# Gate bias in nine rows, one transpose for the conv state, the sample tokens' output product in fp32, and an output norm in two passes

## The chip, the cores and the metric

The kernel runs on one core of one Trainium2 chip. The metric is the device time of one launch in microseconds (us); the figure to compare is the median of several launches of the compiled program. TensorE (PE) multiplies matrices out of SBUF into PSUM, VectorE (DVE), ScalarE (ACT) and GpSimd (POOL) work on tiles, and SyncE (SP) issues all of this kernel's transfers (DMA), one queue for the whole program.

## The reference

One step of one decoder layer with D = 1024, for a prompt of 512 tokens and for 8 sample sequences of 4 tokens with caches. Branch A is dilated window attention, branch B a gated delta rule with a short convolution ahead of it. What matters for this change:

```python
shift, scale, gate = jnp.split(jax.nn.silu(c) @ w_cond + b_cond, 3, axis=-1)   # c: 1 prompt row, 8 sample rows
h = x * (1 + scale[:, None]) + shift[:, None]
... = h @ w_in                                    # one projection; a part of it is qkv_b, 3 x 1024 columns
...
qkv_ext = concatenate([conv_state, qkv_b], axis=1)            # conv_state: 3 rows ahead of the tokens (zeros for the prompt)
qkv = silu(sum(qkv_ext[:, i:i + n] * w[i] for i in range(4)))
new conv_state = qkv_ext[:, -3:]                  # outputs conv_prompt (3, 3072) and conv_sample (8, 3, 3072)
...
merged = sigmoid(ga) * (ya @ w_branch_a) + sigmoid(gb) * (yb @ w_branch_b)
r = ALPHA * x + gate[:, None] * (merged @ w_out)
mu, var = mean(r), mean((r - mu) ** 2)            # over the 1024 columns of a row
out = (r - mu) * rsqrt(var + LN_EPS) * ln_g + ln_b
```

All arrays are float32.

## The kernel before

**How the order comes about.** The code does not issue instructions as it runs. It records them (`Recorder`), and a planner puts them in an order for each engine: it simulates the engines with a table of costs (`cost`), takes for an engine among the instructions that are ready the one of the lowest rank, then the one recorded first, and at the end `emit` issues everything in that order. That is why each row of the profile has line 724: rows are told apart by the names of their tiles (`out<-in`). A result counts as ready for the plan at its planned end plus `margin` (line 702): 0.1 us behind an instruction, 0.5 us behind a transfer. Pools of buffers decide when a tile can be written again. An instruction with `.at` is not planned ahead of that planned time. `rec.together()` keeps a group of instructions without others between. `rec.either` is a copy that goes to VectorE or ScalarE, whichever the plan has free.

**The stream.** The projection `h @ w_in` and the two branch products are a list of jobs, each with 128 columns of weights. The tokens (512 + 32 = 544) are the moving operand, in two halves of 272 columns. Weights and activations are split into a high and a low part (`hi`, `lo`; `hhi`, `hlo`) of the type fp32r, and each product is three: hi x hi, hi x lo, lo x hi, all added up in the PSUM tile `pp`. `wt` is a loaded weight tile, `ext` the evacuated result of a conv job. The other work of the layer runs as threads beside the stream, and its matmuls are put between those of the stream.

**The gate.** `gate_rows` (line 2007) computes the gate's third of `silu(c) @ w_cond + b_cond` in two halves of 512 columns. The weights `wg` come in eight loads. The product goes to `Y`; a matmul with the constant `sel` makes 73 rows of the 9 (prompt and 8 samples) in `pd`: those 9, then the samples' rows for their 32 tokens, twice. `grow` is loaded with the bias in 73 rows, VectorE adds `pd`, and `grow` is stored in DRAM (`dg`). At the end `gp` (the prompt's row on 128 partitions) and `gs` (64 x 1024, the samples' rows) are read back from `dg`.

**The conv state and the delta rule.** For each of 8 heads three conv jobs (q, k, v) run in the stream. Each copies its last three columns of the prompt and of the samples into `cx`; `delta_blocks` (line 1185) transposes `cx` in three pieces of 35 columns, copies the result to `crow`, and stores it with four transfers (one to `conv_p`, three to `conv_s`). In the same function scale factors of a head go through DRAM: `rrow` is stored as `dr` and read back by all partitions as `rb`. VectorE multiplies q and k of the head in `KQ` by scale factors from there, and TensorE transposes `KQ`. `rc` is a small tile of such factors that TensorE transposes earlier. `dblk`, `Ls`, `dtz` and `Tc` are later stations of the same head by way of DRAM (`Tb` is what `dtz` is stored from). `bias` is a tile of the position bias of the attention, which ScalarE exponentiates after its load (`bias_p`). `dO` and `rbo` are the same kind of round trip for the delta rule's output; `S` is its state, `KP` and `PTa` operands of the sample tokens' delta rule and attention, `slab` rows of the cache. `out_kv_s` are copies of caches from DRAM to DRAM, 16 rows at a time.

**The output.** The product with `w_out` runs over two halves of 512 columns (`wo0h`, `wo0l` and `wo1h`, `wo1l`: the halves' high and low parts, split from `wo`). For the prompt the merged activations are stationary (`mhi`, `mlo`), 128 tokens at a time, three products for each of 8 pieces; the last token tile goes in two steps of 256 columns. For the samples `ms` holds the high parts of 32 tokens and the low ones side by side, 64 stationary columns, and both are multiplied by `wo..h` and `wo..l`. In each half the order is: samples (tile 4), then token tiles 0 to 3. VectorE forms `r` = gate x product + ALPHA x `x` (the loaded piece `xr`), its statistics (`bn`, `mv`), and then the norm in five passes over `r` with the norm's weights `lng` and `lnb`, partly in one operation (`SCALAR_TENSOR_TENSOR`: subtract and multiply, or multiply and add) over 512 columns, or 768 for the last tile, partly in three single steps for the rest.

Of the kernel before, what the change touches and what calls it, by code (L numbers as in the profile page):

```python
# [19 lines left out]
D = 1024  # L20
KT = 8
# [224 lines left out]
class Recorder:  # L246
# [455 lines left out]
    def margin(self, p, op):  # L702
        return 0.1 if p.transfer is None else 0.5
# [73 lines left out]
def body(ctx, tc, io):  # L777
# [359 lines left out]
    def conv_job(h, s):  # L1137
# [4 lines left out]
        def begin():  # L1142
            if s == 1:
                hd.cx = dl.tile([128, 3, 35], F32, name="cx")
# [6 lines left out]
        def evac(n, ps):  # L1151
# [13 lines left out]
            ge.tensor_copy(cx[:, s, 0:3], ext[:, 512:515])  # L1165
            ge.tensor_copy(cx[:, s, 3:].rearrange("p (t b) -> p b t", b=8), es[:, :, 3:7])
# [18 lines left out]
    def delta_blocks(h):  # L1185
# [821 lines left out]
    def gate_rows():  # L2007

        sel = cst[:, CCOLS["selc"][0]:CCOLS["selc"][0] + 73]
        for n in range(2):  # L2010
            w = slice(512 * n, 512 * n + 512)
            wc = [op.tile([128, NT], F32, name="wg", tag="o")[:, 0:512] for _ in range(KT)]
            for k in range(KT):
                d = sp.dma_start(wc[k], io["w_cond"][128 * k:128 * k + 128, 2 * D + 512 * n:2 * D + 512 * n + 512])
                d.at = GATES[0] + (GATES[1] - GATES[0]) * (KT * n + k) / (2 * KT)
# [118 lines left out]

    def load_out(n):

        for k in range(0, KT, 2):
            raw = wraw.tile([128, 2, 512], F32, name="wo", tag="wraw")
# [208 lines left out]
```

## Time and profile before

| | |
|---|---|
| median of 3 runs | 930.28 us (930.02 to 931.19) |
| the profiled execution's own time | 931.52 us |
| its span, first to last instruction | 929.7 us |
| granted TensorE clock, mean | 0.988 |
| busy: TensorE, VectorE, ScalarE, GpSimd | 95%, 72%, 50%, 7% |
| matmul records, instructions in all | 8066, 20669 |
| moved | 238.37 MB, mean 256 GB/s |

The profile is of one execution. Times in its rows are us from the start of the span; the rows of a timeline give start, length, engine, operation, out<-in with shapes, and in brackets how long the engine stood idle just before and what it waited for. In the page's second part each digit stands for a fortieth of the span, 23.2 us, in tenths. Rows of the list of waits read: engine, tile it works on, what released it, total idle time, number of waits, longest. The chain of waits goes back from the last instruction and is printed in order of time. fp32 matmuls show more than one record for each instruction.

### The profile page before, as it was taken

The page shows a single profiled execution, that of the slowest core. Times are in us where ns is not written, and L with a number is a line of the kernel's source. Part 1 is how long each engine was busy: PE and PEld are TensorE (multiplying, and loading weights), DVE is VectorE, ACT ScalarE, POOL GpSimd, SP SyncE. Part 2 cuts the span into 40 slices and gives each one's busy share as a digit, 9 for nine tenths or more (in the row PEclk, how much of TensorE's full clock was granted, in tenths as well). Part 3 has the DMA queues.
Part 4 walks back from the last instruction along what each step waited for, and adds up shares of the span by engine and source line. Part 5 has one row for each costly group of instructions (what it writes and reads, how often), then busy time and mean ns, then how long its engine had stood idle before and what let it go on. Part 6 is the DMA issues. An engine that isn't in the chain of part 4 may idle for free.

```text
span 929.7 us, 20669 instructions
## 1 busy us (share of the span) xinstructions
PE 887.5 (95%) x8066; PEld 824.7 (89%) x8066; DVE 670.6 (72%) x1421; ACT 466.8 (50%) x1124; POOL 62.7 (7%) x176
## 2 busy tenths in 40 slices
PE   4899999899999999999999999999999999999995
PEld 1599998788999899989999989998899999989884
DVE  0574434575567999679998875637789799978768
ACT  0365468563568753568764666553352222234421
POOL 0120000010100100010110100102010000000000
PEclk9799999999999999999999999999999999999998
DMA  9678686575787969887888875549969899986713
GB/s 356 231 215 263 197 283 215 203 244 172 234 279 257 298 204 316 266 270 257 289 266 292 279 244 169 189 154 304 337 212 349 276 418 420 356 306 206 265 54 113
DMA packets 106766, 238.37 MB, mean 256 GB/s; under 512 B 31030, under 2 KB 62272, under 8 KB 103980
## 3 DMA queue, kind: packets, MB, share of 16 engines
q1 hardware_dynamic: 106668, 237.05, 75.4%
q8 instruction: 63, 1.03, 0.4%
q14 instruction: 35, 0.29, 0.1%
HBM read 220.69 MB, written 104.00 MB: 349 GB/s over the span
## 4 chain that ended last, share of the span: by engine, by line
PE 78%; DMA 11%; DVE 6%; ACT 2%; SPq 2%; issue 1%; DVEq 0%; ACTq 0%
PE pp L724 61%; PE pg L724 7%; PE pd L724 6%; PE pb L724 3%; DMA grow<-in_b_cond 2%; DMA wc<-in_w_cond 2%; SPq L724 2%; DMA out_kv_s<-in_cache 1%; DMA dtz<-Tb 1%; DMA bias<-in_bias_p 1%; DVE lo L724 1%; DMA rbo<-dO 1%; DVE acc L724 1%; DMA slab<-in_ks 1%; DVE r L724 1%
## 5 line engine op out<-in xcount | busy, mean ns | idle before, releaser
L724 PE MATMUL pp<-hhi,hi 128*128 128x272 f32 x1408 | 416.7, 296 | 7.6 <-ACT ext L724 3.1
L724 PE MATMUL pp<-hhi,lo 128*128 128x272 f32 x1408 | 416.6, 296 | 0.0
L724 PE MATMUL pp<-hlo,hi 128*128 128x272 f32 x1408 | 414.7, 295 | 0.2 <-DVE small L724 0.2
L724 PEld LDWEIGHTS pp<-hhi,hi 128*128 128x128 f32 x1408 | 267.2, 190 | 13.2 <-issue 4.1
L724 PEld LDWEIGHTS pp<-hlo,hi 128*128 128x128 f32 x1408 | 267.1, 190 | 2.9 <-issue 1.4
L724 PEld LDWEIGHTS pp<-hhi,lo 128*128 128x128 f32 x1408 | 266.7, 190 | 3.3 <-issue 2.1
L724 ACT ACTIVATE hi<-wt 128x1024 fp32r<-128x1024 f32 (+1 forms) x104 | 106.8, 1027 | 158.5 <-PE pp L724 117.9
L724 DVE TENSOR_TENSOR lo<-wt,hi 128x1024 fp32r<-128x1024 f32 (+1 forms) x104 | 122.8, 1180 | 57.2 <-ACT hi L724 51.0
L724 DVE SCALAR_TENSOR_TENSOR acc<-ext,cw,acc 128x568 f32<-128x568 f32 x72 | 57.7, 801 | 0.9 <-ACT acc L724 0.4
L724 ACT ACT_TABLE_LOAD x38 | 48.8, 1283 | 13.5 <-DMA cT<-in_cT 7.9
L724 DVE TENSOR_TENSOR slab<-slab 128x512 f32<-128x512 f32 (+1 forms) x66 | 42.9, 670 | 8.5 <-DMA slab<-in_ks 5.6
L724 DVE TENSOR_REDUCE slab<-slab 128x8 f32<-128x512 f32 (+2 forms) x66 | 43.0, 661 | 0.3
L724 ACT ACTIVATE zt<-pp 128x272 f32<-128x272 f32 x48 | 18.7, 390 | 38.2 <-PE pp L724 35.9
L724 PE MATMUL pp<-ybl,hi 128*128 128x272 f32 x128 | 36.9, 289 | 0.0
L724 PE MATMUL pp<-ybh,hi 128*128 128x272 f32 x128 | 36.9, 288 | 0.0
L724 PE MATMUL pp<-ybh,lo 128*128 128x272 f32 x128 | 36.6, 286 | 0.0
L724 ACT ACTIVATE P<-P,st 128x256 f32<-128x256 f32 (+1 forms) x64 | 31.2, 489 | 9.0 <-DVE st L724 8.8
L724 POOL COPY cx<-ext 128x3 f32<-128x3 f32 (+1 forms) x48 | 22.9, 506 | 117.7 <-ACT ext L724 117.7
L724 DVE TENSOR_TENSOR tmp<-Ls,Tb 32x15 f32<-32x15 f32 (+7 forms) x120 | 23.1, 193 | 5.5 <-DMA Ls<-dblk 2.2
L724 DVE CUSTOM_DVE_ANT_0 P<-pg,bias 128x256 f32<-128x256 f32 (+1 forms) x64 | 23.1, 400 | 5.4 <-PE pg L724 5.4
L724 ACT ACTIVATE spare<-pp 128x272 f32<-128x272 f32 (+1 forms) x32 | 16.0, 501 | 21.1 <-PE pp L724 21.0
L724 DVE TENSOR_TENSOR Tb<-Tb,tmp 32x15 f32<-32x15 f32 (+7 forms) x120 | 23.4, 195 | 4.1
(388 smaller groups left out, 1529.6 us busy)
## 6 DMA issues: line engine op xcount, KB each, us to landing
out_kv_s<-in_cache SPq DMA_DIRECT2D x144, 512.0 KB
wt<-in_w_in SPq DMA_DIRECT2D x88, 512.0 KB
out_kv_s<-in_cache SPq DMA_DIRECT2D x24, 496.0 KB
wc<-in_w_cond SPq DMA_DIRECT2D x8, 1024.0 KB
slab<-in_ks SPq DMA_DIRECT2D x32, 256.0 KB
slab<-in_vs SPq DMA_DIRECT2D x32, 256.0 KB
kv<-in_ks SPq DMA_DIRECT2D x16, 512.0 KB
kv<-in_vs SPq DMA_DIRECT2D x16, 512.0 KB
```

The source lines that it names most:

```text
L724: getattr(real[x.engine], x.name)(*map(arg, x.args), **{k: arg(v) for k, v in x.kw.items()})
```

## The change

Five things change, and the planner gives a new order for everything.

1. *Gate.* The bias comes as 9 rows (`brow`) into a tile that VectorE or GpSimd has set to zero before, loaded ahead of the weights `wg`. VectorE adds the product to it, the `sel` matmul repeats the sum as 73 rows, and these are copied to `grow` (`either`) and stored in `dg` as before.
2. *Conv state.* `cx` is [128, 81], one transpose, one copy, two stores.
3. *Margin.* A transfer's result counts as ready 1.0 us after its planned landing instead of 0.5.
4. *Samples' output product.* `ms` is [128, 8, 32] in fp32, copied by GpSimd. The product runs in one piece between the two halves: 8 x 4 matmuls of 32 stationary and 256 moving columns, each of the four on 32 rows of `pp` and its own column group of TensorE, with `w_out` unsplit. For this the first half of `w_out` is loaded a second time (2 MB, into the buffers `hi` and `lo`), and of the second half the loaded raw tiles `wo` are kept. `gs` is read back as four pieces of 32 x 256.
5. *Output norm.* Two passes over a tile: subtract the mean and multiply by `lng` over 1024 columns, then multiply by the reciprocal deviation and add `lnb`, in two pieces of 512. The work of the last tile gets the rank -2 and so goes ahead of others that are ready.

```diff
     def margin(self, p, op):
-        return 0.1 if p.transfer is None else 0.5
+        return 0.1 if p.transfer is None else 1.0
...
-            ge.tensor_copy(cx[:, s, 0:3], ext[:, 512:515])
-            ge.tensor_copy(cx[:, s, 3:].rearrange("p (t b) -> p b t", b=8), es[:, :, 3:7])
+            ge.tensor_copy(cx[:, s:9:3], ext[:, 512:515])
+            ge.tensor_copy(cx[:, 9:81].rearrange("p (b t u) -> p u b t", t=3, u=3)[:, s], es[:, :, 4:7])
...
-        for s in range(3):
-            pe.transpose(pt[0:35, s * 128:(s + 1) * 128], cx[:, s, :], ident)
-        crow = dl.tile([35, 3, 128], F32, name="crow", bufs=1)
-        rec.either(crow, cols128(pt)[0:35, 0:3])
-        cols = lambda o: o.rearrange("t (s h d) -> h t s d", h=8, d=128)[h]
-        sp.dma_start(cols(io["conv_p"]), crow[0:3])
-        for t in range(1, 4):
-            sp.dma_start(cols(io["conv_s"][:, t - 1, :]), crow[3 + 8 * t:11 + 8 * t])
+        pe.transpose(pt[0:81, 0:128], cx, ident)
+        crow = dl.tile([81, 128], F32, name="crow", bufs=1)
+        rec.either(crow, pt[0:81, 0:128])
+        sp.dma_start(io["conv_p"].rearrange("t (s h d) -> h (t s) d", h=8, d=128)[h], crow[0:9])
+        sp.dma_start(io["conv_s"].rearrange("b t (s h d) -> h (b t s) d", h=8, d=128)[h], crow[9:81])
...
         for n in range(2):
             w = slice(512 * n, 512 * n + 512)
+            row = op.tile([128, NT], F32, name="brow", tag="o")[:, 0:512]
+            at = GATES[0] + (GATES[1] - GATES[0]) * n / 2
+            ge.memset(row, 0.0).at = at - 2.0
+            sp.dma_start(row[0:9], io["b_cond"][:, 2 * D + 512 * n:2 * D + 512 * n + 512].to_broadcast([9, 512])).at = at
...
-            Y = op.tile([128, NT], F32, name="Y", tag="o")[:, 0:512]
-            se.activation(Y, ps[n], AF.Copy)
-            rows = op.tile([128, NT], F32, name="grow", tag="o")[0:73, 0:512]
-            sp.dma_start(rows, io["b_cond"][:, 2 * D + 512 * n:2 * D + 512 * n + 512].to_broadcast([73, 512]))
+            ve.tensor_add(row, ps[n], row)
             yield 3.0
             p = pd()
-            pe.matmul(p[0:73], sel, Y, start=True, stop=True)
-            ve.tensor_add(rows, rows, p[0:73])
+            pe.matmul(p[0:73], sel, row, start=True, stop=True)
+            rows = op.tile([128, NT], F32, name="grow", tag="o")[0:73, 0:512]
+            rec.either(rows, p[0:73])
             sp.dma_start(dg[:, w], rows)
...
-    ms = al.tile([128, 8, 64], F32R, name="ms")
+    ms = al.tile([128, 8, NS], F32, name="ms")
-    gs = al.tile([64, D], F32, name="gs")
+    gs = al.tile([128, 256], F32, name="gs")
...
-    sp.dma_start(gs, dg[9:73])
+    for q in range(4):
+        sp.dma_start(gs[32 * q:32 * q + 32], dg[9:41, 256 * q:256 * q + 256])
...
+    for k in range(0, KT, 2):
+        name = ("hi", "lo")[k // 4]
+        plain[0, k] = wsp.tile([128, 2, 512], F32R, name=name, tag=name).bitcast(F32)
+        sp.dma_start(plain[0, k], out_rows(0, k))
...
+    def norm_out(tt):
+        rows = slice(0, 128) if tt < 4 else slice(0, 32)
+        q = r[tt][rows]
+        mv = o2.tile([128, 4], F32, name="mv")[rows]
+        ve.bn_aggr(mv[:, 0:2], bn[tt][rows].rearrange("p a b -> p (a b)"))
+        se.activation(mv[:, 2:3], mv[:, 1:2], AF.Sqrt, bias=eps5[rows, 0:1])
+        ve.scalar_tensor_tensor(q, q, mv[:, 0:1], lng[rows], op0=OP.subtract, op1=OP.mult)
+        ve.reciprocal(mv[:, 2:3], mv[:, 2:3])
+        out = io["y_p"][128 * tt:128 * tt + 128] if tt < 4 else io["y_s"]
+        for w in (slice(0, 512), slice(512, 1024)):
+            ve.scalar_tensor_tensor(q[:, w], q[:, w], mv[:, 2:3], lnb[rows, w], op0=OP.mult, op1=OP.add)
+            sp.dma_start(out[:, w], q[:, w])
+
+    def samples_out():
+        xr = [load_x(4, n) for n in range(2)]
+        po = pp()
+        with rec.together():
+            for k in range(KT):
+                for q in range(4):
+                    n, c = divmod(256 * q, 512)
+                    pe.matmul(po[32 * q:32 * q + 32, 0:256], ms[:, k], plain[n, k // 2 * 2][:, k % 2, c:c + 256],
+                              start=(k == 0), stop=(k == 7), tile_position=(0, 32 * q))
...
+        for tt in range(4):
+            xr, q = load_x(tt, n), r[tt]
             step = 256 if tt == 3 else 512
             for c in range(512 * n, 512 * n + 512, step):
                 po = product_out(tt, c, c + step)
                 w = slice(c, c + step)
+                rec.rank = -2 * (n and tt == 3)
+                ve.scalar_tensor_tensor(q[:, w], po, 0.5, gp[:, w], op0=OP.mult, op1=OP.mult)
...
+            if n:
+                rec.rank = -2 * (tt == 3)
+                norm_out(tt)
+                rec.rank = 0
```

Where the rows of the new order stand, engine by engine at the places that matter. The first is SyncE's queue around the first half of the gate (numbers behind a name, as in `dr_2022`, tell tiles of one name apart). Before:

```order
L724 DMA grow<-in_b_cond 73x512
L724 DMA dO<-orow 128x512
L724 DMA wg<-in_w_cond 128x512 x2
L724 DMA out_kv_s<-in_cache 16x8192
L724 DMA dg<-grow 73x512
L724 DMA wg<-in_w_cond 128x512
L724 DMA bias<-in_bias_p 128x1024
L724 DMA out_kv_s<-in_cache 16x8192
L724 DMA dr_2022<-rrow 8x128
L724 DMA wt<-in_w_in 128x1024
L724 DMA wg<-in_w_cond 128x512
L724 DMA out_kv_s<-in_cache 16x8192
```

and `rb` is the next row. After:

```order
L724 DMA bias<-in_bias_p 128x1024
L724 DMA out_kv_s<-in_cache 16x8192
L724 DMA wg<-in_w_cond 128x512 x2
L724 DMA brow<-in_b_cond 9x512
L724 DMA dr_1969<-rrow 8x128
L724 DMA wt<-in_w_in 128x1024
L724 DMA wg<-in_w_cond 128x512
L724 DMA dg<-grow 73x512
L724 DMA out_kv_s<-in_cache 16x8192
L724 DMA rb<-dr_1969 128x1024
```

The bias of the first half now stands some 30 rows earlier (the `brow` here is the second half's); `bias` and `dr` have moved ahead of the store `dg`, and `rb` stands second behind it.

The same queue around the second half. Before:

```order
L724 DMA grow<-in_b_cond 73x512
L724 DMA dr_2478<-rrow 8x128
L724 DMA wt<-in_w_in 128x1024
L724 DMA rb<-dr_2478 128x1024
L724 DMA out_kv_s<-in_cache 16x8192
L724 DMA out_kv_p<-spare 128x128
L724 DMA dg<-grow 73x512
L724 DMA out_kv_s<-in_cache 16x8192
L724 DMA dtz<-Tb 16x16x16 x2
```

After:

```order
L724 DMA out_kv_s<-in_cache 16x8192
L724 DMA dr_2470<-rrow 8x128
L724 DMA dg<-grow 73x512
L724 DMA rb<-dr_2470 128x1024
L724 DMA out_kv_s<-in_cache 16x8192
L724 DMA wt<-in_w_in 128x1024
```

The store of 73 rows stood behind `rb`, and now stands between `dr` and `rb`.

TensorE between the two halves of the output product. Before, the second half begins with the samples' 16 matmuls of 512 columns:

```order
L724 MATMUL pp<-wo0h,mhi 128x256
L724 MATMUL pp<-wo0l,mhi 128x256
L724 MATMUL pp<-wo0h,mlo 128x256
L724 MATMUL pp<-wo1h,ms 64x512
L724 MATMUL pp<-wo1l,ms 64x512
L724 MATMUL pp<-wo1h,ms 64x512
```

After, with the first half's reloaded pieces under the names `hi` and `lo` and the second half's raw ones under `wo`:

```order
L724 MATMUL pp<-wo0h,mlo 128x256
L724 MATMUL pp<-hi,ms 32x256 x2
L724 MATMUL pp<-wo,ms 32x256 x2
L724 MATMUL pp<-hi,ms 32x256 x2
L724 MATMUL pp<-wo,ms 32x256 x2
L724 MATMUL pp<-hi,ms 32x256 x2
```

The samples' matmuls now stand here only, 32 in a row, and the first half begins with the prompt's tokens.

VectorE at the very end. The numbers of `r` tell the token tiles apart: before, `r_11513` is tile 2 and `r_11546` tile 3; after, `r_11448` and `r_11475`. Before:

```order
L724 SCALAR_TENSOR_TENSOR r_11546<-pp,gp 128x256
L724 TENSOR_TENSOR r_11513<-r_11513,lnb 128x512
L724 TENSOR_TENSOR r_11546<-r_11546,xr 128x256
L724 BN_STATS bn_11557<-r_11546 128x6
L724 BN_AGGR mv<-bn_11557 128x2
L724 SCALAR_TENSOR_TENSOR r_11546<-r_11546,mv,lng 128x768
L724 RECIPROCAL mv<-mv 128x1
L724 TENSOR_SCALAR r_11546<-r_11546,mv 128x256
L724 SCALAR_TENSOR_TENSOR r_11546<-r_11546,mv,lnb 128x512
L724 TENSOR_TENSOR r_11546<-r_11546,lng 128x256
L724 SCALAR_TENSOR_TENSOR r_11546<-r_11546,mv,lnb 128x256
L724 TENSOR_TENSOR r_11546<-r_11546,lnb 128x256
```

After:

```order
L724 SCALAR_TENSOR_TENSOR r_11475<-pp,gp 128x256
L724 BN_AGGR mv<-bn_11545 128x2
L724 TENSOR_TENSOR r_11475<-r_11475,xr 128x256
L724 SCALAR_TENSOR_TENSOR r_11448<-r_11448,mv,lng 128x1024
L724 BN_STATS bn_11560<-r_11475 128x6
L724 RECIPROCAL mv<-mv 128x1
L724 BN_AGGR mv<-bn_11560 128x2
L724 SCALAR_TENSOR_TENSOR r_11448<-r_11448,mv,lnb 128x512
L724 SCALAR_TENSOR_TENSOR r_11475<-r_11475,mv,lng 128x1024
L724 RECIPROCAL mv<-mv 128x1
L724 SCALAR_TENSOR_TENSOR r_11448<-r_11448,mv,lnb 128x512
L724 SCALAR_TENSOR_TENSOR r_11475<-r_11475,mv,lnb 128x512 x2
```

Before, one operation of tile 2 stands behind the last tile's final read of PSUM (the first row), and eleven of tile 3 from that read on; after, five of tile 2 and eight of tile 3.

More of the change, by code (lines that the diff above doesn't have):

```diff
@@ L1143, in begin @@
             if s == 1:
-                hd.cx = dl.tile([128, 3, 35], F32, name="cx")
+                hd.cx = dl.tile([128, 81], F32, name="cx")
                 hd.stc = dl.tile([128, 3, 8, 3], F32, name="stc")
@@ L2133, in body, with out_rows @@
         ve.tensor_sub(yal[j], ya[j], yah[j].bitcast(F32))
+    plain = {}
+    def out_rows(n, k):
+        return io["w_out"][k * 128:k * 128 + 256, 512 * n:512 * n + 512].rearrange("(a p) c -> p a c", a=2)
     def load_out(n):
         for k in range(0, KT, 2):
-            raw = wraw.tile([128, 2, 512], F32, name="wo", tag="wraw")
-            sp.dma_start(raw, io["w_out"][k * 128:k * 128 + 256, 512 * n:512 * n + 512].rearrange("(a p) c -> p a c", a=2))
+            raw = (wraw if n == 0 or k < 6 else o1).tile([128, 2, 512], F32, name="wo", **({"tag": "wraw"} if n == 0 or k < 6 else {}))
+            sp.dma_start(raw, out_rows(n, k))
+            plain[n, k] = raw
             se.activation(wo[n][0][:, k:k + 2], raw, AF.Copy)
@@ L2177, in body @@
     sp.dma_start(lnb, io["ln_b"].to_broadcast([128, D]))
-    lo4 = o1.tile([32, 512], F32, name="lo4")
+    for k in range(0, KT, 2):
+        name = ("hi", "lo")[k // 4]
+        plain[0, k] = wsp.tile([128, 2, 512], F32R, name=name, tag=name).bitcast(F32)
+        sp.dma_start(plain[0, k], out_rows(0, k))
     eps5 = o1.tile([128, 1], F32, name="eps5")
@@ L2187, in product_out @@
         po = pp()[:, 0:c1 - c0]
-        if tt < 4:
-            for k in range(KT):
-                for i, (a, b) in enumerate(parts(k)):
-                    pe.matmul(po, a[:, 128 * tt:128 * tt + 128], wo[n][b][:, k, w],
-                              start=(k == 0 and i == 0), stop=(k == 7 and i == 2))
-            return po
-        for k in range(KT):
-            for b in range(2):
-                pe.matmul(po[0:64], ms[:, k], wo[n][b][:, k, w], start=(k == 0 and b == 0), stop=(k == 7 and b == 1))
@@ L2198, in product_out @@
-        return po[0:64]
-    for n in range(2):
-        for tt in (4, 0, 1, 2, 3):
-            pr_ = slice(0, 128) if tt < 4 else slice(0, 32)
-            gate = gp if tt < 4 else gs
-            xr = o2.tile([128, 512], F32, name="xr")
-            sp.dma_start(xr[pr_], io["x"][128 * tt:128 * tt + 128 if tt < 4 else NT, 512 * n:512 * n + 512])
-            se.activation(xr[pr_], xr[pr_], AF.Copy, scale=ALPHA)
-            q = r[tt][pr_]
-            last = n == 1 and tt == 3
+        for k in range(KT):
+            for i, (a, b) in enumerate(parts(k)):
+                pe.matmul(po, a[:, 128 * tt:128 * tt + 128], wo[n][b][:, k, w],
+                          start=(k == 0 and i == 0), stop=(k == 7 and i == 2))
@@ new lines, in product_out, with load_x @@
+        return po
+    def load_x(tt, n):
+        rows = slice(0, 128) if tt < 4 else slice(0, 32)
+        xr = o2.tile([128, 512], F32, name="xr")
+        sp.dma_start(xr[rows], io["x"][128 * tt:128 * tt + 128 if tt < 4 else NT, 512 * n:512 * n + 512])
+        se.activation(xr[rows], xr[rows], AF.Copy, scale=ALPHA)
+        return xr[rows]
+    def norm_out(tt):
+        rows = slice(0, 128) if tt < 4 else slice(0, 32)
+        q = r[tt][rows]
[8 more added lines that the diff above has]
+            sp.dma_start(out[:, w], q[:, w])
@@ new lines, in samples_out @@
+    def samples_out():
+        xr = [load_x(4, n) for n in range(2)]
+        po = pp()
+        with rec.together():
+            for k in range(KT):
+                for q in range(4):
+                    n, c = divmod(256 * q, 512)
+                    pe.matmul(po[32 * q:32 * q + 32, 0:256], ms[:, k], plain[n, k // 2 * 2][:, k % 2, c:c + 256],
+                              start=(k == 0), stop=(k == 7), tile_position=(0, 32 * q))
+        q = r[4][0:32]
+        for b in range(4):
+            rows = slice(32 * b, 32 * b + 32)
+            ve.scalar_tensor_tensor(q[:, 256 * b:256 * b + 256], po[rows, 0:256], 0.5, gs[rows], op0=OP.mult, op1=OP.mult)
+        for n in range(2):
+            w = slice(512 * n, 512 * n + 512)
+            ve.tensor_add(q[:, w], q[:, w], xr[n])
+            ve.bn_stats(bn[4][0:32, n, :], q[:, w])
+        norm_out(4)
@@ L2212, in body @@
                 w = slice(c, c + step)
[L2213 to L2238 removed]
+                rec.rank = -2 * (n and tt == 3)
+                ve.scalar_tensor_tensor(q[:, w], po, 0.5, gp[:, w], op0=OP.mult, op1=OP.mult)
+                ve.tensor_add(q[:, w], q[:, w], xr[:, c - 512 * n:c - 512 * n + step])
+                ve.bn_stats(bn[tt][:, c // step, :], q[:, w])
+                rec.rank = 0
+            if n:
+                rec.rank = -2 * (tt == 3)
+                norm_out(tt)
+                rec.rank = 0
     ox.close()
```

32 lines of the change are left out of this document (3 added, 29 removed).

## Prediction

> **What bounds the kernel now.** I read the page first (busy shares and slices), then the chain of waits, then the list of who waited for whom, and last the timelines around the four places that the change touches.
>
> ```profile
> PE 887.5 (95%) x8066; PEld 824.7 (89%) x8066; DVE 670.6 (72%) x1421; ACT 466.8 (50%) x1124; POOL 62.7 (7%) x176
> ...
> PE   4899999899999999999999999999999999999995
> ...
> DMA  9678686575787969887888875549969899986713
> ...
> 728.91 45.97 PE pp L724 x365
> ```
>
> TensorE is busy from the second slice to the last; the transfers are full in a few slices only. The last row is a stretch of the chain: 365 matmuls of 272 columns in 45.97 us, 0.126 us each, one behind the other. So the kernel is a stream of TensorE work with the scheduler's other work put between: a microsecond of TensorE work removed, or of its stalls, is a microsecond of time, until about 919 us; behind that VectorE and the last stores decide.
>
> The stalls that matter here lie around the two gate products:
>
> ```profile
> 155.49 9.90 DMA grow<-in_b_cond
> 168.38 9.11 DMA bias<-in_bias_p
> 204.43 10.96 DMA grow<-in_b_cond
> ...
> DVE grow L724 <- DMA grow<-in_b_cond: 9.1, 2, 6.0
> ACT bias L724 <- DMA bias<-in_bias_p: 6.8, 3, 5.1
> ...
> 165.47 0.68 DVE L724 TENSOR_TENSOR grow<-grow,pd 73x512 f32<-73x512 f32 x1 [6.02 <-DMA grow<-in_b_cond]
> ...
> 166.19 0.25 SPq L724 DMA_DIRECT2D dg<-grow  x1
> ...
> 207.73 0.27 SPq L724 DMA_DIRECT2D dr<-rrow  x1
> ...
> 215.65 0.34 SPq L724 DMA_DIRECT2D rb<-dr  x1
> ...
> 166.84 0.27 PE L724 MATMUL pb<-cst,rc 128*8 128x128 f32 x1 [1.52 <-DVE rc L724]
> ...
> 179.54 0.40 PE L724 MATMUL pp<-hhi,hi 128*128 128x272 f32 x1 [2.39 <-ACT ext L724]
> ...
> 221.41 0.92 PE L724 MATMUL pb<-KQ 128*128 128x256 f32 x3 [1.74 <-DVE KQ L724]
> ```
>
> The load of the bias into 73 rows (`grow`) is issued only when the product is done, takes 9.90 and 10.96 us for 146 KB, and VectorE stands behind it for 6.02 and some 3.1 us (9.1 in two waits). SyncE's store `dg` waits for VectorE, and what is queued behind it goes late: `bias`, which then takes 9.11 us and holds ScalarE for 5.1. At the second one `dr` leaves 3.3 us behind `grow` and `rb`, which reads it back, only 8 us later. TensorE's three stalls at these places are 1.52, 2.39 and 1.74 us, together 5.65.
>
> **The change, part by part.** The sum is made of differences against the profiled execution (span 929.7 us; its own time 931.52 lies 1.2 above the median of the runs, 930.28) and is taken from the median.
>
> *Sample tokens' output product.*
>
> ```profile
> 867.02 0.39 PE L724 MATMUL pp<-wo0h,ms 128*64 128x512 f32 x1
> 867.25 0.40 PE L724 MATMUL pp<-wo0l,ms 128*64 128x512 f32 x1
> ...
> 545.54 1.05 PE L724 MATMUL pg<-slab,PTa 128*32 128x256 f32 x16
> 546.52 0.25 PE L724 MATMUL pd<-W,Xc 32*32 32x16 f32 x8
> ...
> 191.17 1.10 PE L724 MATMUL pb<-KQ 128*128 128x256 f32 x4
> ...
> 867.00:920.00 53.00, 52.57 (x274) 1.00 0.38 133
> ...
> 880.93 1.06 ACT L724 ACTIVATE wo1h<-wo 128x1024 fp32r<-128x1024 f32 x1 [0.60 <-DMA wo<-in_w_out]
> ...
> 897.05 0.39 PE L724 MATMUL pp<-wo1h,mhi 128*128 128x512 f32 x1
> ...
> 919.35 0.29 PE L724 MATMUL pp<-wo1h,mlo 128*128 128x256 f32 x1
> ```
>
> Removed: 32 matmuls that start 0.23 us apart, 7.4 us. Added: 32 fp32 matmuls of 32 x 256 on four column groups. The `PTa` row is the same shape on the same four groups: 8 instructions (16 records) from 545.54 to 546.52, 0.98 us, so 32 take 3.9. The other end, had the groups not overlapped, is the fp32 product on the full array: two instructions (4 records) in 1.10, or 17.6 for 32; the `PTa` row excludes it. Gain 3.5. The four reloads of w_out (2 MB) run beside the four token tiles of the first half, 22.6 us (the second half's, from 897.05 to 919.64), in a stage whose transfers are at a share of 0.38 and 133 GB/s (the window's row: DMA share and GB/s are its last two numbers); 2 MB at the page's mean rate of 256 GB/s is 8 us. Cost 0; without that cover up to 8. In SyncE's queue they stand ahead of the second half's last weights, which were split at 880.93; 8 us later is 889, and the samples' product asks for that piece at about 867.0 + 22.6 + 2.9 = 892.5: 3.5 us are left. The small copies of `ms` go from ScalarE and VectorE to POOL, which is 7% busy: 0.
>
> *One transpose for the conv state.*
>
> ```profile
> 91.06 0.49 PE L724 MATMUL pb<-cst,cx 128*35 128x128 f32 x3
> 91.30 0.37 PE L724 MATMUL pp<-hhi,lo 128*128 128x272 f32 x1
> 91.51 0.29 PE L724 MATMUL pp<-hhi,hi 128*128 128x272 f32 x1
> ```
>
> From 91.06 to 91.51 three transposes and one matmul take 0.45 us; less the matmul's 0.126 the three are 0.32, 0.11 each. Two fewer in each of 8 heads: 16 x 0.11 = 1.7 us off TensorE. The new one has 81 stationary columns and the same 128 moving ones; I take the same 0.11 (ends: 0.03, its spacing inside the row, and 0.32). Sixteen stores fewer and a shorter PSUM copy lie beside TensorE: 0.
>
> *Gate bias in nine rows.* The load leaves before the product, and VectorE's addition of 512 columns takes the place of ScalarE's copy; the three stalls lose their cause, 5.65 us. What is late next: the store of 73 rows stays, and in SyncE's new order `rb` is the first load behind it that a chain waits for, in both halves, where before it was `bias` once and `dtz` once. Behind `rb` VectorE's product `KQ` waits, behind that (in order) the conv sums, and then TensorE.
>
> ```profile
> L724 SPq DMA_DIRECT2D bias<-in_bias_p x4: 328/352/934, 67.4 to 453.7; - x4
> L724 ACT ACTIVATE bias<-bias x4: 1042/1058/1060, 75.0 to 458.3; 128x1024 f32<-128x1024 f32 x4
> ```
>
> How long a 512 KB load is held by that store: the last `bias` load was used 4.6 us after its issue (453.7, 458.3), the one behind the store landed after 9.11, so about 4.5 us (below: 9.11 less 7.6 of the first load, 1.5). Against it stands the planned distance: in TensorE's new order 78 stream matmuls (9.8 us) lie between the transpose of `rc` and the first `KQ` product of that head, 106 before; in the second half 79 and 76. Ends for the new stalls: 0, and twice 2.39. I take twice the 1.6 that is the mean of 1.52 and 1.74, because there too VectorE was the late one: 3.3 back. Gain 2.4, between 5.65 and 0.9.
>
> How 146 KB come to need 10 us: the page's mean of 256 GB/s is 16 for one of 16 engines, and 146 KB at 16 GB/s are 9.1 us, so the row reads as one engine's work. [...]
>
> *The margin of the planner* (a transfer's result counted on 1.0 us after its planned landing, 0.5 before) removes no instruction; it moves the consumers of transfers later in each engine's order, earlier or later by up to some 85 of the stream's matmuls.
>
> ```profile
> 656.52 0.41 PE L724 MATMUL pb<-S,KP 128*32 128x128 f32 x2 [1.60 <-DMA S<-in_state_delta]
> ...
> PE pg L724 <- DMA rbo<-dO: 0.5, 1, 0.5
> PE pd L724 <- DMA Tc<-dtz: 0.4, 1, 0.4
> ```
>
> TensorE's direct waits for transfers outside the front and the gates are these three, 2.5 us. Each can shrink by 0.5 (0.4 for the last): 1.4 at best. Against that, a new order makes stalls of its own; one as large as the largest above, 2.39, is the other end. Taken: gain 1.0, between +2.5 and -2.4.
>
> *Output norm in two passes, last tile first.*
>
> ```profile
> 919.86 0.74 DVE L724 SCALAR_TENSOR_TENSOR r<-r,mv,lnb 128x512 f32<-128x512 f32 x1
> ...
> 921.12 0.42 DVE L724 SCALAR_TENSOR_TENSOR r<-pp,gp 128x256 f32<-128x256 f32 x1
> ...
> 922.97 0.26 DVE L724 BATCH_NORM_AGGREGATE mv<-bn 128x2 f32<-128x24 f32 x1
> 923.26 1.02 DVE L724 SCALAR_TENSOR_TENSOR r<-r,mv,lng 128x768 f32<-128x768 f32 x1
> 924.20 0.16 DVE L724 RECIPROCAL mv<-mv 128x1 f32<-128x1 f32 x1
> ...
> 926.11 0.42 DVE L724 TENSOR_TENSOR r<-r,lnb 128x256 f32<-128x256 f32 x1
> ```
>
> VectorE ends 6.9 us behind TensorE (926.53 against 919.64), the span 3.2 behind that. From 919.86 on stand 14 rows, 7.3 us by their durations, which overlap a little. A pass over 512 columns takes 0.74, over 768 1.02, so over 1024 1.3; a tile's norm falls from five passes to three. But in the new order 13 rows stand from the last tile's first read of PSUM to the end, and five of them belong to tile 2, whose 1024-wide and two 512-wide passes are put between those of tile 3. By durations: four of 256 columns or less around the statistics (0.42 + 0.42 + 0.43 + 0.26), tile 2's 0.26 + 1.3 + 0.16 + 0.75 + 0.75, tile 3's 1.3 + 0.16 + 0.75 + 0.75, together 7.7, or 7.3 with the overlap of before. So the tail is 0.4 longer behind TensorE's end and not shorter; I take +0.3, between -0.7 (tile 2 done in time) and +1.0.
>
> Sum: -3.5 - 1.7 - 2.4 - 1.0 + 0.3 = -8.3, so 922.0 us.
>
> **Rivals.**
> *The store of 73 rows takes the gate's gain back.* For it: the 9.11 us of `bias` behind that store, and `rb` right behind it twice. Against: `rb` has the 9.8 us of stream work as cover. Gate part 0: 924.4, and 925.4 with the margin's gain gone too.
> *All stalls go.* `rb` lands in time and the margin takes the direct waits: -3.5 - 1.7 - 5.65 - 1.4 + 0.3 = -12.0, 918.3; a new order with less stalls of its own takes it to 916.
> *Slower: the margin lengthens each head's chain of transfers.* A head of the delta rule passes six transfers one after the other (`dr`, `rb`, `dblk`, `Ls`, `dtz`, `Tc`), 0.5 us later each, 3 us a head, 24 for eight. Heads wait for each other's buffers; if the stream of projections had to stop for them, this would decide as soon as 8.3 of the 24 reached TensorE, and half of it gives 934.0. Against: TensorE is at 9 tenths in nearly every slice, so the stream covers these chains, and in the new order the last two heads' steps stand 7 to 60 matmuls earlier.
> *The reloads come late.* If the samples' product waits for them, up to 8 us go: 930.0, no change that shows. Against: the 3.5 us left.
>
> **How the numbers follow.** Forecast 0.60 (own range 918 to 925), store 0.19, all stalls 0.12, reloads 0.04, longer chains 0.05. The range of 916.5 to 927.5 holds the first three but for their edges. A measurement of this kernel tells about 0.2%, 1.9 us, from no change. Faster by more than that (under 928.4): the first three, 0.91; within it: the reloads, 0.04; slower: the chains, 0.05.
>
> **What would show it.** Right: `ms` matmuls 32-wide, taking about 3.9 us at one place; no wait of VectorE for `grow`; `cx` eight times; VectorE's wait for `rb` at two places and a TensorE stall of 1 to 2 us before `KQ`. Wrong: if the span from the first `wo0h` matmul to the first of `wo1h` is not 26 us; if the tail behind TensorE's last matmul is not 9.5 to 11 us; or if TensorE waits between 250 and 860 us differ from before by more than 3 us, for then the new order decides and not the parts.

## Result and profile after

The changed kernel takes 921.57 us (median of 4 runs, 918.99 to 922.36) against 930.74 for the kernel before; the ratio is 0.9894, with a 95% interval from 0.9871 to 0.9918. The forecast was 922.0. The number was met, but not by its terms alone: the gate's gain did not come, and the new order of the instructions gave more than the forecast had for it. So the hit is in part luck; the experiments below show which terms held.

The page of the changed kernel, busy times and the slices of TensorE, its granted clock and the transfers:

```profile
span 919.7 us, 20682 instructions
...
PE 883.6 (96%) x8082; PEld 823.5 (90%) x8082; DVE 663.6 (72%) x1399; ACT 459.5 (50%) x1115; POOL 68.5 (7%) x186
...
PE   4899999999999999999999999999999999989995
...
DMA  9778785765788879896889865648969899985933
```

The chain of waits still runs through TensorE, but the gate stands in it again, with another transfer: `rb`.

```profile
167.21 11.04 DMA rb<-dr
...
208.77 9.19 DMA rb<-dr
...
851.29 55.27 PE pp L724 x352
```

`grow` and `bias`, which were in the chain before, are gone from it. In their place the load of `rb` takes 11.04 and 9.19 us, each time issued behind the store of 73 rows. The timeline around the first of them, SyncE's queue, then VectorE, then TensorE's three longest stalls behind the front of the program:

```profile
166.30 0.24 SPq L724 DMA_DIRECT2D dg<-grow  x1
166.60 0.52 SPq L724 DMA_DIRECT2D out_kv_s<-in_cache  x1
167.21 0.53 SPq L724 DMA_DIRECT2D rb<-dr  x1
...
178.27 1.23 DVE L724 TENSOR_TENSOR KQ<-KQ,rb 128x1024 f32<-128x1024 f32 x1 [2.36 <-DMA rb<-dr]
...
179.55 0.79 PE L724 MATMUL pb<-KQ 128*128 128x256 f32 x1 [2.07 <-DVE KQ L724]
...
219.26 0.70 PE L724 MATMUL pb<-KQ 128*128 128x256 f32 x2 [2.16 <-DVE KQ L724]
...
826.21 0.52 PE L724 MATMUL pp<-yah,hi 128*128 128x272 f32 x2 [2.09 <-ACT yah L724]
```

The first two were forecast (1.6 us each). The third was not foreseen as such: at 826 us TensorE waits for the samples' attention to be finished and converted (`yah`); before, it waited 0.25 us there.

At the output, first the row of the samples' tile `ms` (records, shortest, median and longest duration in ns, first and last start in us), then from the timeline TensorE's next and last row and VectorE's last long ones:

```profile
L724 PE MATMUL pp<-wo,ms x32: 379/379/403, 883.1 to 886.4; 128*32 128x256 f32 x32
```

```profile
886.70 0.50 PE L724 MATMUL pp<-wo1h,mhi 128*128 128x512 f32 x1
...
909.10 0.29 PE L724 MATMUL pp<-wo1h,mlo 128*128 128x256 f32 x1
...
910.23 1.28 DVE L724 SCALAR_TENSOR_TENSOR r<-r,mv,lng 128x1024 f32<-128x1024 f32 x1
...
913.93 2.06 DVE L724 SCALAR_TENSOR_TENSOR r<-r,mv,lnb 128x512 f32<-128x512 f32 x3
```

The product takes 3.6 us at one place (883.1 to 886.7) and nothing waits ahead of it, so the reloads are hidden. VectorE ends at 915.99, 6.6 us behind TensorE (909.39).

Five points on the way through the program, from the traces (us), make the comparison. The rows below the first two are experiments that follow.

| | first product with `yah` | first with `wo0h` | first prompt product of the second half | TensorE's last matmul ends | end |
|---|---|---|---|---|---|
| before | 832.80 | 867.02 | 897.05 | 919.64 | 929.7 |
| changed | 826.21 | 860.63 | 886.70 | 909.39 | 919.7 |
| before, margin alone | 827.77 | 862.01 | 891.78 | 914.35 | 924.4 |
| before, samples' product alone | 833.01 | 866.51 | 893.97 | 916.68 | 927.9 |
| before, norm alone | 834.40 | 868.63 | 898.37 | 920.95 | 929.3 |
| before, transfers of 73 rows split | 825.71 | 859.94 | 889.68 | 912.26 | 922.1 |
| changed, old margin | 828.16 | 862.26 | 888.25 | 910.96 | 919.5 |
| changed, store of 33 rows | 819.27 | 853.92 | 879.99 | 902.68 | 912.4 |

From before to changed: 6.6 us are gained up to the first `yah` product, 0.2 lost behind it, 4.0 gained between the halves, 0.1 lost in the second half, 0.25 lost in the tail: 10.0 in these two profiles, 9.2 by the medians. Profiles of one order differ too: at the first `yah` product the norm alone, whose order is that of before up to there, is 1.6 us later, and a second profile of the changed kernel 1.8 us earlier (824.40). From there on, stretches of one order agree within some 0.6 us, so the losses of 0.1 to 0.25 us say nothing.

### The profile page after: what moved, and what is told of

The parts are those of the page before. It is cut to its first block, busy times and chain, and to the rows that moved or that the text cites. A ratio compares the mean times of both kernels' runs of the same rounds, so it can differ in the third digit from the quotient of the medians.

```text
span 919.7 us, 20682 instructions
## 1 busy us (share of the span) xinstructions
PE 883.6 (96%) x8082; PEld 823.5 (90%) x8082; DVE 663.6 (72%) x1399; ACT 459.5 (50%) x1115; POOL 68.5 (7%) x186
## 4 chain that ended last, share of the span: by engine, by line
PE 86%; DVE 5%; DMA 4%; ACT 2%; SPq 1%; issue 1%; DVEq 0%; POOL 0%; POOLq 0%; ACTq 0%
PE pp L724 67%; PE pg L724 8%; PE pd L724 7%; PE pb L724 4%; DMA rb<-dr 2%; DMA wc<-in_w_cond 1%; SPq L724 1%; DMA dO<-orow 1%; DVE r L724 1%; DVE acc L724 1%; DVE lo L724 1%; DVE xT L724 0%; ACT sq L724 0%; ACT hi L724 0%; DVE KQ L724 0%
## 5 line engine op out<-in xcount | busy, mean ns | idle before, releaser
L724 ACT ACTIVATE ext<-pp 128x272 f32<-128x272 f32 (+2 forms) x72 | 19.9, 315 | 12.7 <-PE pp L724 12.7
L724 PE MATMUL pp<-wc,cs 128*32 128x512 f32 x64 | 13.7, 984 | 12.7 <-DMA wc<-in_w_cond 12.7
```

Of the source, the lines that this page charges most:

```text
L724: getattr(real[x.engine], x.name)(*map(arg, x.args), **{k: arg(v) for k, v in x.kw.items()})
```

## Experiments

All ratios below are against the kernel before, from runs beside it on the same chip, with 95% intervals. Kernels that were run together shared their chip: the changed kernel with its short stores and its transposes; the two margins, the gate and the samples' product alone; the split transfers, the margins of 0.8 and 0.9 and the norm alone.

### The store of 73 rows

The changed kernel again as the level:

> The changed kernel once more, as the level for the three runs beside it. 921.6 us, between 919 and 922.4; its profile should again show two stalls of TensorE ahead of a KQ product of about 2.1 us each and one of about 2.1 us ahead of the first product with yah.

It took 921.42 us (ratio 0.9881, 0.9855 to 0.9907), with the same three stalls (1.81, 2.15, 2.09 us).

In the same order of instructions, the store `dg` sent as rows 0 and 9 to 40 only, which are all that is read, and then as rows 0 and 9 to 72:

```diff
 # when the order is issued, for the two stores of shape (73, 512)
-sp.dma_start(dg[:, w], rows)
+sp.dma_start(dg[0:1, w], rows[0:1])
+sp.dma_start(dg[9:41, w], rows[9:41])      # second kernel: 9:73
```

> The changed kernel in the same order on every engine, but each store dg writes row 0 and rows 9 to 40 only (two transfers, 1 and 32 rows) in place of 73 rows; the other rows are read by nobody. Theory A (the store of 73 rows runs on one DMA engine for 6 us and holds rb, which the KQ product waits for): rb lands in 6 to 7 us instead of 11.0 and 9.2, both KQ stalls of TensorE go (2.1 and 2.2 us), 917.4 us, that is 4 us less than the changed kernel. Rival B (rb is late because of the 512 KB copy out_kv_s and the other loads around it, and the store is only a neighbour): rb stays at 9 us or more, the stalls at about 2 us each, 921.6 us.

> As the one with 33 rows, but rows 0 and 9 to 72 are stored: 65 of the 73 rows, 130 KB of 146. [...] Rival C (it is the bytes of the store, or its rows of 2 KB): 89% of the effect stays, rb at 9 to 11 us, 921 us.

Measured: 914.69 us with 33 rows (0.9809, 0.9783 to 0.9834) and 914.65 with 65 rows (0.9815, 0.9788 to 0.9842). Both `KQ` stalls are gone, and 65 of the 73 rows do the same as 33: it is not the bytes. Theory A of the 33 rows holds in that both stalls go, and it was too small: 6.7 us in place of 4. The windows show why. Columns: length, busy time and instructions of TensorE, its weight loads, VectorE, ScalarE, GpSimd, then the granted clock, the DMA share and GB/s. The stretch of the gate in the changed kernel, and in it the time at the lower clock behind each of its `KQ` stalls:

```profile
150.00:230.00 80.00, 75.57 (x602) 68.59 (x600) 47.84 (x112) 45.67 (x119) 5.65 (x24) 0.96 0.66 213
...
179.51:182.92 3.41, 3.37 (x11) 3.01 (x12) 2.55 (x5) 1.75 (x2) 0.52 (x1) 0.50 0.60 233
...
220.47:223.88 3.41, 3.41 (x15) 3.23 (x14) 0.99 (x3) 0.00 (x0) 0.42 (x2) 0.50 0.66 189
```

and the same stretch with the store of 33 rows:

```profile
150.00:230.00 80.00, 79.78 (x720) 72.96 (x720) 52.06 (x128) 48.61 (x129) 6.62 (x26) 1.00 0.71 233
```

In the changed kernel TensorE is idle for 4.4 us of this stretch, and behind each stall it runs at half the clock for 3.41 us, which by half of that time costs an estimated 1.7 us more each. With the short store 0.2 us are idle, and 720 matmul records fit in the stretch instead of 602. The first `KQ` product of VectorE starts at 175.90 and waits for nothing. The trace's records of single packets show what goes on at the second store: in the changed kernel its 73 packets of 2 KB run one behind the other, most of them 84 ns long, from 209.2 to 216.4 us; with 65 rows the packets run side by side, from 205.8 to 207.3.

The same cause tested in the kernel before, where both the loads `grow` and the stores `dg` have 73 rows. Its order stays, all bytes go to the same places:

```diff
 # when the order is issued, for every transfer of shape (73, 512)
-sp.dma_start(out, in_)
+sp.dma_start(out[0:64], in_[0:64])
+sp.dma_start(out[64:73], in_[64:73])
```

> The kernel before in its own order on every engine, but each load grow and each store dg of 73 rows is issued as two transfers, of 64 and of 9 rows: the same bytes to the same places. [...] Rival B (the load is late because it is issued only when the product is done, whatever its rows): loads of 6 us or more, half of the stalls stay, 928 to 929.

Measured: 923.07 us against 930.89 (0.9915, 0.9898 to 0.9932), a gain of 7.8; the time is 0.9 us below the 924 to 926 that the author had expected of the split, and rival B's 928 to 929 did not come. The stretch of the gate before, and with the split:

```profile
150.00:230.00 80.00, 74.16 (x571) 67.27 (x571) 47.68 (x113) 46.83 (x117) 7.46 (x23) 0.98 0.64 204
```

```profile
150.00:230.00 80.00, 80.00 (x712) 73.43 (x715) 52.74 (x130) 50.64 (x127) 8.01 (x25) 1.00 0.73 235
```

and, from the timeline with the split, VectorE's addition to the first `grow` (lines are shifted by the code put in):

```profile
162.58 0.68 DVE L729 TENSOR_TENSOR grow<-grow,pd 73x512 f32<-73x512 f32 x1 [2.48 <-DMA grow<-in_b_cond]
```

No idle time at all is left on TensorE there (5.8 us before). VectorE still waits 2.5 us for the first `grow`, which TensorE does not feel. In the packet records the 73 packets of the second `grow` load follow one another from 208.7 to 214.9 us before, and run side by side from 201.3 to 203.4 with the split. Splitting these transfers alone gained 7.8 us; the five edits of the change together gained 9.2.

### The gate edit alone

> The kernel before with the gate edit alone: bias in nine rows ahead of the product. In its order the first store dg stands ahead of rb, the second behind rb and ahead of the load Tc, and no stream matmul lies between the samples' last attention product and the first with yah (24 before). Theory A (the three stalls of 5.65 us at the gate go, one KQ stall of about 2.1 us with a low clock behind it comes, and the yah stall of 3 us or more comes with its low clock): 929 to 932, no gain that shows. Rival B (the gate edit is worth its 2.4 to 5.65 us by itself): 925 to 928.

The edit is the `gate_rows` part of the diff, on the kernel before. Measured: 931.09 us (0.9991, 0.9971 to 1.0012), theory A: no gain that shows. Its store of 73 rows is still there. The window of the gate:

```profile
150.00:230.00 80.00, 74.95 (x635) 68.21 (x634) 47.38 (x111) 43.41 (x113) 8.87 (x26) 0.98 0.66 215
```

TensorE is idle for 5.05 us there, 5.84 before, and the stalls at the gate have been traded for one of 3.99 us ahead of the `KQ` product; another of 2.2 us came ahead of a later head's `KQ` (367 us), and stalls of 1.5 and 1.6 us at the samples' last attention step and `yah`.

### The margin

> The kernel before with the margin alone changed (1.0 us in place of 0.5). Theory A (the margin as forecast takes direct waits for transfers, and in the changed kernel it is the margin that removed about 6 us of small stalls between 290 and 660 us, but also that left only 10 stream matmuls in place of 24 between the samples' last attention product and the first product with yah; here 13 are left): stalls between 250 and 660 us shrink by 4 to 6 us, a stall of about 2 us appears ahead of yah with a lower clock behind it, together 927 to 930. Rival B (the small stalls went by the re-planning of the other parts): no change between 250 and 660, the yah stall costs its 3 to 4 us, 933 to 934.

```diff
-        return 0.1 if p.transfer is None else 0.5
+        return 0.1 if p.transfer is None else 1.0
```

Measured: 925.76 us (0.9934, 0.9919 to 0.9948), 6.0 less, more than either theory gave. The signs of theory A came (fewer small stalls, a new one at `yah`), its time did not. What the margin takes away, by the windows from 230 to 690 us, of before and of the margin alone, and then TensorE's row at `yah` with the margin alone:

```profile
230.00:690.00 460.00, 453.82 (x4708) 427.63 (x4706) 352.33 (x840) 282.12 (x722) 43.22 (x116) 1.00 0.78 256
```

```profile
230.00:690.00 460.00, 457.45 (x4665) 433.84 (x4664) 357.75 (x845) 281.59 (x720) 42.47 (x114) 1.00 0.78 255
```

```profile
827.77 0.52 PE L724 MATMUL pp<-yah,hi 128*128 128x272 f32 x2 [2.09 <-ACT yah L724]
```

TensorE's idle time there falls by 3.6 us, from 6.2 to 2.5, and the foreseen stall of 2.1 us comes at `yah`. TensorE's direct waits for transfers give 1.3 of the 3.6; they fall from 2.5 to 1.2. Another 2.4 are three stalls of the kernel before at 299, 308 and 314 us, and its chain of waits leads them back to one load of the cache rows `slab`. The first, read upwards from TensorE: it waits for ScalarE's `P`, that for VectorE, and VectorE for `slab`. The last two rows are the other two stalls:

```profile
297.00 0.69 DVE L724 TENSOR_TENSOR slab<-slab 128x512 f32<-128x512 f32 x1 [2.81 <-DMA slab<-in_ks]
...
298.67 0.51 ACT L724 ACTIVATE P<-P,st 128x256 f32<-128x256 f32 x1 [0.93 <-DVE st L724]
...
299.32 0.44 PE L724 MATMUL pg<-cst,P 128*128 128x128 f32 x2 [0.81 <-ACT P L724]
...
307.74 0.65 PE L724 MATMUL pb<-cst,KQ 128*128 128x128 f32 x4 [0.87 <-DVE KQ L724]
...
314.01 0.39 PE L724 MATMUL pp<-hhi,hi 128*128 128x272 f32 x1 [0.71 <-ACT ext L724]
```

VectorE's waits for transfers of the attention and the delta rule, before:

```profile
DVE slab L724 <- DMA slab<-in_ks: 5.6, 3, 2.8
DVE Xc L724 <- DMA Tc<-dtz: 5.5, 2, 2.9
...
DVE slab L724 <- DMA slab<-in_vs: 2.3, 1, 2.3
DVE tmp L724 <- DMA Ls<-dblk: 2.2, 1, 2.2
...
DVE kv L724 <- DMA kv<-in_ks: 1.6, 1, 1.6
```

and with the margin alone:

```profile
DVE slab L724 <- DMA slab<-in_vs: 1.7, 2, 1.5
...
DVE Xc L724 <- DMA Tc<-dtz: 1.4, 2, 0.9
...
DVE slab L724 <- DMA slab<-in_ks: 0.9, 1, 0.9
...
DVE kv L724 <- DMA kv<-in_ks: 0.8, 1, 0.8
```

In these rows 17.2 us became 4.8. All of VectorE's waits for transfers, those for the gate, `rb` and a weight tile included, fell from 32.0 to 22.5 us only, because at the gate the margin alone brings a loss: the second `rb` now stands right behind the second store of 73 rows, VectorE waits 7.4 us for it (0.7 before), and TensorE is idle for 5.72 us at one place. In the window of the gate its idle time is 5.7 us, as before (5.8).

The idle times do not add up to the gain, though. TensorE from one and the same matmul of the stream near 80 us to the first with `wo0h` (length, busy time and records, then clock, DMA share and GB/s), before and with the margin alone:

```profile
80.34:867.02 786.68, 772.42 (x7360) 1.00 0.79 265
```

```profile
80.31:862.01 781.70, 769.66 (x7360) 0.99 0.80 267
```

Of the 5.0 us gained here, idle time (length less busy time) gives 2.2, and the lower clock takes 1.8 back: it is half for 3.41 us before and for three times that with the margin alone, in part during a stall. The other 4.6 us are busy time at the full clock, for the same matmuls. Busy time hides small delays: a row of the stream lasts 0.29 us and the next one starts 0.126 behind it, so by estimate (0.29 less 0.126) a start can come some 0.16 us late without idle time. In the samples' product alone, the norm alone and the split transfers, all in the order of before up to here, this busy time is within 1.4 us of before; in the gate edit alone, planned anew, it is 4.0 less. So it goes with the order; which delays went is not shown.

The other direction, the changed kernel with the old margin:

> The changed kernel with the old margin of 0.5 us. In its order 25 stream matmuls lie between the samples' last attention product and the first product with yah (10 in the changed kernel), and the second store dg stands behind rb and ahead of dtz, the first still ahead of rb. Theory A (the margin removes small stalls behind transfers and costs the yah stall): the yah stall of 2.1 us and the low clock behind it go (3 to 4 us), the second KQ stall goes (2.1 us and its low clock), and stalls of 4 to 6 us come back elsewhere: 919 to 922. Rival B (the margin did nothing between 250 and 660 us): 915 to 916.

Measured: 921.66 us (0.9897, 0.9881 to 0.9912), the same as the changed kernel. The `yah` stall is gone, as expected from the 25 matmuls of distance; but between 230 and 690 us TensorE is idle for 7.1 us (the window), with one stall as long as 3.8 (the timeline), and at the gate one `KQ` stall of 3.2 us has taken the place of two of 2.1:

```profile
230.00:690.00 460.00, 452.88 (x4642) 429.01 (x4642) 356.02 (x843) 275.53 (x716) 45.83 (x114) 0.99 0.78 255
```

```profile
675.15 0.56 PE L724 MATMUL pp<-hhi,hi 128*128 128x272 f32 x1 [3.82 <-DVE zt L724]
```

By the five points it is 1.95 us behind the changed kernel at the first `yah` product, and takes 1.8 of them back in the tail (8.5 us from TensorE's end against 10.3). So the margin is worth 6 us on the kernel before and nothing on the changed one: what it moves depends on the order that it meets.

Two values between, with the store of 33 rows, were to unite both gains:

> The changed kernel with the store dg as 1 and 32 rows and the margin at 0.8 us. In its order 27 stream matmuls lie between the samples' last attention product and the first with yah (10 at a margin of 1.0). Theory A (the gap in matmuls decides the yah stall, and a margin of 0.8 keeps most of the small stalls away): no yah stall over 0.5 us and no low clock behind it, 3 to 4 us less than with the margin of 1.0 and the same store (914.7): 910.5 to 912, idle time of TensorE between 230 and 690 us at 1.5 to 3 us. Rival B (each new order makes a stall of its own of 2 us or more somewhere else): 914 to 917.

> The same at a margin of 0.9 us, with 21 stream matmuls in that gap. Theory A: a yah stall under 1 us, 911 to 912.5. Rival B as for 0.8: 914 to 917.

Measured: 915.29 us at 0.8 (0.983, 0.9812 to 0.9849) and 916.19 at 0.9 (0.9839, 0.9822 to 0.9857); 914.69 was the level at 1.0, on another chip, and the intervals overlap. Theory A fell; the times are rival B's. At 0.8 the `yah` stall is gone, and another of 2.35 us has come for a transfer that had been early enough (window and timeline):

```profile
230.00:690.00 460.00, 455.47 (x4629) 431.04 (x4628) 358.13 (x838) 276.90 (x712) 46.12 (x114) 1.00 0.77 255
```

```profile
631.21 0.82 PE L729 MATMUL pg<-cst,rbo 128*128 128x128 f32 x4 [2.35 <-DMA rbo<-dO]
```

At 0.9 a `yah` stall of 1.43 us is left (21 matmuls of distance), and idle time between 230 and 690 us is 5.9 us. The distance in matmuls does go with the `yah` stall: 24 and 25 gave at most 0.25, 27 none, 21 gave 1.43, 13 and 10 gave 2.09; with none, in the gate edit alone, it was 1.61 behind the other of 1.49. That is one stall out of many, and each order has its own.

### The samples' output product alone

> The kernel before with the samples' output product alone: fp32 on four column groups between the halves, reload of the first half of w_out, gs in four pieces; norm in five passes as before. Theory A (32 matmuls in 3.8 us in place of 7.4, reloads hidden): 3.5 us less, 926.8 to 927.5, the tail behind TensorE's last matmul 10 us as before. Rival B (reloads or the copies of ms collide with the branch products): 929 or more, with a wait ahead of the first matmul with ms.

Measured: 929.67 us against 931.8 (0.9975, 0.9962 to 0.9988), 2.1 less by the medians. That is outside theory A's range and inside rival B's, but rival B's sign, a wait ahead of the first matmul with `ms`, is absent. The product itself takes 3.6 us, as forecast (890.4 to 894.0), and from the first `yah` product to the first prompt product of the second half 3.3 us are gained; but with the norm of five passes TensorE's end is followed by 11.2 us instead of 10.1, which takes 1.1 back.

### The norm alone

> The kernel before with the output norm alone changed: two passes over each tile and the last tile's work first. Up to the output the order is that of before. Theory A (as forecast: fewer passes, but work of tile 2 stands between those of tile 3): from TensorE's last matmul to the end 9.4 to 11 us (10.1 before), no change that shows, 929.6 to 932. Rival B (the norm is the bound of the tail and two passes less take 1 to 1.5 us off): tail at 8.5 to 9 us.

Measured: 929.77 us (0.9987, 0.9972 to 1.0001); the interval just includes no change, and the time is in theory A's range. From TensorE's end to the program's end, however, it is 8.35 us, 1.7 less than before, which is rival B's sign and a little more. Here tile 2 is done ahead of tile 3's last read of PSUM, and in the changed kernel with the old margin (8.5) all but one pass of it; in the changed kernel all its passes stand behind that read (10.3).

### The transposes

> The changed kernel in the same order, but the one transpose of cx is issued three times for each of 8 heads (16 instructions more, the number that the change removed). Theory A (TensorE is the bound there, 0.11 us each): 1.7 us more than the changed kernel, 923.3. Rival (they follow one another at 0.03 us, or lie in stalls): under 0.6 us more, 921.6 to 922.2.

```diff
-pe.transpose(pt[0:81, 0:128], cx, ident)
+for _ in range(3): pe.transpose(pt[0:81, 0:128], cx, ident)
```

Measured: 921.94 us against the level of 921.42, with ratios of 0.9884 (0.9858 to 0.991) and 0.9881: their intervals are wider than the 1.7 us in question, so the times settle nothing. At the place itself the price shows, one transpose in the changed kernel and three here:

```profile
94.40 0.27 PE L724 MATMUL pb<-cst,cx 128*81 128x128 f32 x1
94.43 0.37 PE L724 MATMUL pp<-hhi,lo 128*128 128x272 f32 x1
94.64 0.29 PE L724 MATMUL pp<-hhi,hi 128*128 128x272 f32 x1
```

```profile
94.51 0.49 PE L725 MATMUL pb<-cst,cx 128*81 128x128 f32 x3
94.76 0.37 PE L725 MATMUL pp<-hhi,lo 128*128 128x272 f32 x1
94.97 0.29 PE L725 MATMUL pp<-hhi,hi 128*128 128x272 f32 x1
```

From the transpose to the second matmul behind it 0.24 us became 0.46: 0.22 for two, 1.8 us for eight heads.

## Why the prediction was right, and where it was not

**Samples' product, -3.5: right.** 3.6 us at one place, reloads hidden, and 4.0 us less between the first `wo0h` and the first prompt product of the second half (26.07 against 30.03; the forecast said 26).

**Transposes, -1.7: right at the spot** (1.8), not separable in the whole time.

**Gate, -2.4: wrong, the gate gained about nothing.** The forecast took stalls of 5.65 us away and put twice 1.6 back. Two steps failed. The new `KQ` stalls were sized too small: they are 2.07 and 2.16 us, together 1.0 more. And a stall was priced by its idle time alone: a stretch of half the clock behind it (3.41 us at 0.50) costs an estimated 1.7 us more, once at the gate before and twice in the changed kernel (once in its second profile). Idle time and clock together, in the window of 80 us, the gate costs 5.84 + 1.7 = 7.5 us before, 4.43 + 3.4 = 7.8 changed, 0.2 with the store of 33 rows. The changed kernel's second profile had 4.17 + 1.7 = 5.9, so the gain is between -0.3 and 1.7. The rival on the store of 73 rows named this outcome, with `rb` right behind that store, and it was given 0.19. With 64 + 9 rows in the kernel before, and with 1 + 64 in the changed one, TensorE's idle time in that window went from 5.84 to 0.00 us and from 4.43 to 0.21, at 100% and 89% of the bytes. That 73 rows are one engine's work is the author's estimate: the packets of such a transfer run one behind the other, but their records name no engine. The forecast's 9.1 us for one engine met the load's 9.90 and 10.96 us for a wrong reason: in the second load the packets took 6.2 us, and the first of them started 4.3 us behind the issue.

**Margin, -1.0: wrong in size.** The step that failed counted only TensorE's direct waits for transfers (1.4 at best). These did fall, by 1.3 us with the margin alone. But alone it gave 6.0 us, beyond the forecast's own upper end of 2.5: stalls behind other engines went too, and most of the gain is busy time that the same matmuls no longer needed, which no list of waits shows.

**Tail, +0.3: right** as far as it can be told, 10.06 to 10.31, with tile 2's passes between tile 3's as forecast; 0.25 us is less than tails of one order differ (9.72 with the store of 33 rows). That the same edit takes 1.7 off where the order lets it is what the forecast's lower end (-0.7) did not reach.

So 922.0 held a gate gain that did not come. What made up for it is in the new order as a whole. TensorE in the changed kernel, from the matmul near 80 us to the first `wo0h`:

```profile
80.72:860.63 779.91, 770.89 (x7345) 0.99 0.80 267
```

That is 6.8 us less than before (8.3 in the second profile). Idle time gives 5.2 of it (4.7), the lower clock takes 3.4 back (1.7), and 4.9 (5.2) are busy time at the full clock, of which the transposes are 1.8. The other 3 us stand in no term of the forecast. The check that the forecast set itself, TensorE's waits between 250 and 860 us differing by more than 3 us, came out at its edge: idle time there is 8.1 us before, 4.6 in the changed kernel and 5.4 in its second profile.

Not settled: which small delays of TensorE went with the new order, and the margin's part in the changed kernel. Alone the margin is worth 6.0, on top of the other four nothing, and each order has its own stalls; single terms do not add up. The conv state's edit was not run alone.

The best version that ran is the changed kernel with the store of 33 or 65 rows, 914.7 us.

## What to carry to other kernels

Look at the row count of every transfer that stands in front of something urgent in a shared queue: two transfers of 64 and 9 rows in place of one of 73 were worth 7.8 us here, more than any of the five edits. Price a stall of TensorE of about 2 us with the clock that follows it (here half for 3.41 us or twice that behind 17 of 20), from the windows behind it, and look through the engine named as releaser to what that engine waited for. Where rows overlap, compare busy time for the same matmuls as well: idle time misses the small delays (4.6 us of busy time with the margin alone). In a kernel whose order a planner sets, no edit of one place is only that: compare the same points of the program, and give a forecast of re-planning a width of several us in both directions.

## What the runs showed of the hardware

In all these traces the granted clock of TensorE is either full (1.00) or half (0.50), and between the front of the program and the tail it is half for 3.41 us or twice that. Such a stretch comes with most stalls of TensorE of about 2 us. In the changed kernel it begins at 179.51 us behind a stall of 2.07 us, at 220.47 behind one of 2.16, and at 828.05 behind the `yah` stall of 2.09:

```profile
828.05:831.46 3.41, 3.39 (x15) 2.99 (x14) 1.76 (x3) 1.31 (x2) 0.00 (x0) 0.50 0.40 154
```

It doesn't follow every time. In the 14 profiles, 17 of the 20 stalls of 2 us or more behind the front have such a stretch, which begins during the stall or up to 2.5 us behind it, and 4 of 18 stalls between 1 and 2 us. In the level run beside the experiments, the same order, the first `KQ` stall (1.81 us) was followed by a clock of 1.00 and the second (2.15 us) by half; with the transposes issued three times, `KQ` stalls of 2.07 and 2.19 us had no lower clock behind them, nor had stalls of 1.52, 1.74 and 1.60 us in the kernel before; one of 1.54 us with the split transfers had. So stalls of one length are followed by either clock (2.07 us by half in the changed kernel, by full with the transposes issued three times), and what decides between them is not shown.
